# The head of a two-layer hybrid trunk as a written-out schedule, on one core

## The chip, the core and the metric

One Trainium2 chip, one of its cores. The metric is the device time of one execution, in microseconds (us). The core has a matrix engine (TensorE, PE in the profile), VectorE (DVE), ScalarE (ACT), GpSimd (POOL) and SyncE (SP), which issues all the transfers here. Each engine takes its instructions in the order in which they stand in its own queue; between engines they wait on semaphores.

## What is computed

Two layers over 256 tokens of width 1024, in float32. Each layer normalizes, makes one wide projection (9304 columns), runs three mixers on its parts (gated linear attention, sparse attention with an indexer, differential attention), projects each branch, merges them by gates and adds an output projection to the stream. x is 1 x 256 x 1024, DEPTH is 2, w_in is 1024 x 9304 a layer. y_a, y_b and y_c are the mixers' outputs, g the gates:

```python
def _rms(x, g=None):
    xf = x.astype(F32)
    y = xf * lax.rsqrt(jnp.mean(xf * xf, axis=-1, keepdims=True) + EPS)
    if g is not None:
        y = y * g.astype(F32)
    return y.astype(x.dtype)

def reference(x, norm_g, w_in, gla_wa2, gla_ba, gla_norm_g, dsa_qn_g, dsa_kn_g, diff_qn_g, diff_kn_g,
              diff_lq1, diff_lk1, diff_lq2, diff_lk2, w_br, w_out):
    B, T, _ = x.shape
    for l in range(DEPTH):
        h = _rms(x, norm_g[l])
        proj = h @ w_in[l]
        (gq, gk, gv, ga, gz, bq, bk, bv, iq, ik, iw, bz,
         cq, ck, cv, cz, gate) = jnp.split(proj, SPLIT_AT, axis=-1)
...
        merged = (g[:, :, 0] * (y_a @ w_br[l, 0])
                  + g[:, :, 1] * (y_b @ w_br[l, 1])
                  + g[:, :, 2] * (y_c @ w_br[l, 2]))
        x = x + merged @ w_out[l]
    return x
```

## The kernel before

**Tiles and products.** The 256 tokens are two tiles of 128 (t = 0, 1). A product in float32 is made of three products of split operands: each operand is a rounded part (hi) and a rest (lo), and `mm3` (L182) issues hi·hi, lo·hi and hi·lo, lines 183 to 185, into one PSUM tile of 128x512. Eight k tiles of 128 make up the depth of 1024, so a block of 512 columns takes 24 products for one t.

**Weights.** They come in 184 units (92 a layer) of 128x1024 float32, 512 KB: two k tiles of one block of 512 columns, so a block is four units. `Stream.need` (L137) issues the transfer of a unit into one of five `raw` buffers, and at L145 ScalarE copies it to `whi` and VectorE subtracts to get `wlo` (six buffers each). `need` runs up to 21 units ahead of its use; buffers coming free set when a transfer starts. The blocks go in the order of ORDER: bq, cq, ck, and so on.

**The head.** Ten idle products on zeros (WARM, L344) run first on PE. SP issues the two halves of x for t = 0 and the identity with the norm gains (`eyeg`, L350). For each t, `sumsq` (L208) squares and sums both halves on ScalarE; `norm_in` (L210) makes v on VectorE, its power -0.5 on GpSimd (L213), scales each half of x to h on VectorE (L217), transposes it on PE in four 128x128 pieces into one PSUM bank `hps` (L220), and copies each piece out: ScalarE writes hTh with the gain (L224), VectorE subtracts to hTl (L225). There are two banks for one t, k tiles 0 to 3 and 4 to 7. The first two units are asked for behind the head of t = 0 (FIRST), x of t = 1 behind them. `proj_first` (L254) does bq for t = 0, then two units of cq for t = 0 (AHEAD1), then bq for t = 1, then the rest of cq.

**What sets the order.** The code is written in this sequence, but a list scheduler behind it puts each engine's queue in an order of its own from its estimates of durations, within dependences. `tc.add_manual_dep` adds an order between two instructions without a semaphore; `ws.hold` (L128) uses it to keep the split of unit 3 of a layer behind the last copy of t = 0. Small tasks of the mixers (`Flow`) are put in between at counted places: `qk_task` normalizes bq's rows (L266 to L271, "qn") and transposes them (L278, "qkT"); `small_task` holds the indexer's keys and weights (L422 to L433, "ikh", "ikl", "iw", "iws"). `constants` (L312) makes masks, gains and scalars.

Of the kernel before, what the change touches and what calls it, by code (L numbers as in the profile page):

```python
# [65 lines left out]
def trunk(ctx: ExitStack, tc: tile.TileContext, x_in, units, wsmall, eye, pack, ptmp, wa2b, out):  # L66
# [57 lines left out]

    class Stream:
        def __init__(self):
            self.made, self.splits, self.after = [], [], {}
# [8 lines left out]

        def need(self, i, ahead=None):  # L137
            ahead = BUFS["ahead"] if ahead is None else ahead
            while len(self.made) < min(L * NUNIT, i + 1 + ahead):
                j = len(self.made)  # L140
                raw = wp.tile([P, 1024], F32, tag="raw", bufs=BUFS["raw"], name=nm("raw"))
                nc.sync.dma_start(raw, units[j])
                hi = wp.tile([P, 1024], F32R, tag="whi", bufs=BUFS["wt"], name=nm("whi"))
                lo = wp.tile([P, 1024], F32R, tag="wlo", bufs=BUFS["wt"], name=nm("wlo"))
                self.splits.append((A.activation(hi, raw, AF.Copy), V.tensor_sub(lo, raw, hi.bitcast(F32))))  # L145
                if j in self.after:
                    self.hold(j, self.after[j])
                self.made.append((hi.rearrange("p (k n) -> p k n", k=2), lo.rearrange("p (k n) -> p k n", k=2)))
# [61 lines left out]
    def norm_in(l, t):  # L210
        v, r = tiny(1, "v"), tiny(1, "r")
        V.scalar_tensor_tensor(v, ss[t][:, 0:1], EPS, ss[t][:, 1:2], op0=OP.add, op1=OP.add)
        G.tensor_tensor(r, v, half[:, :1], op=OP.pow)  # L213
        tt = slice(t * P, t * P + P)
        for hf in range(2):
            h = w2([P, 512], F32, "h")
            V.tensor_scalar_mul(h, x[:, t, HV[hf]], r)  # L217
            ps = at([P, 4, P], "hps")
            for j in range(4):
                TE.transpose(ps[:, j], h[:, j * P:(j + 1) * P], ident)  # L220
            for j in range(4):
                k = 4 * hf + j
                g = gT[:, l * KD8 + k:l * KD8 + k + 1]
                e = (A.activation(hTh[:, k, tt], ps[:, j], AF.Copy, scale=g),  # L224
                     V.scalar_tensor_tensor(hTl[:, k, tt], ps[:, j], g, hTh[:, k, tt].bitcast(F32),  # L225
                                            op0=OP.mult, op1=OP.subtract))
# [709 lines left out]
```

## Time and profile before

| | us |
|---|---|
| median of three timed runs | 612.82 |
| the three runs | 612.48, 612.82, 613.51 |
| the profiled execution's own time | 613.26 |
| its span in the profile | 611.5 |
| PE busy | 604.2 (99%) |
| VectorE busy | 434.1 (71%) |
| ScalarE busy | 354.0 (58%) |
| GpSimd busy | 63.0 (10%) |

The profiled execution took 613.26 us, of which the profile's span covers 611.5; the other 1.8 us lie around it. PE is busy nearly always, so what it does not do is read from single stretches: the list of what PE waited for, busy time by stretch with the granted clock beside it (1.00 is 2.4 GHz, 0.50 is 1.2 GHz), and each engine's timeline of the first tens of microseconds. PE's matmuls are pipelined: a duration of 0.39 us with starts 0.23 us apart means that the rate is 0.23.

### The profile page before, as it was taken

The page shows a single profiled execution, that of the slowest core. Times are in us where ns is not written, and L with a number is a line of the kernel's source. Part 1 is how long each engine was busy: PE and PEld are TensorE (multiplying, and loading weights), DVE is VectorE, ACT ScalarE, POOL GpSimd, SP SyncE. Part 2 cuts the span into 40 slices and gives each one's busy share as a digit, 9 for nine tenths or more (in the row PEclk, how much of TensorE's full clock was granted, in tenths as well). Part 3 has the DMA queues.
Part 4 walks back from the last instruction along what each step waited for, and adds up shares of the span by engine and source line. Part 5 has one row for each costly group of instructions (what it writes and reads, how often), then busy time and mean ns, then how long its engine had stood idle before and what let it go on. Part 6 is the DMA issues. An engine that isn't in the chain of part 4 may idle for free.

```text
span 611.5 us, 8711 instructions
## 1 busy us (share of the span) xinstructions
PE 604.2 (99%) x3180; PEld 507.3 (83%) x3180; DVE 434.1 (71%) x709; ACT 354.0 (58%) x612; POOL 63.0 (10%) x93
## 2 busy tenths in 40 slices
PE   7999999999999999999999999999999999999997
PEld 4788888898899888888878888889888988888886
DVE  5888657777989756648587776676888976575571
ACT  6778855766536754443466787576755555544430
POOL 2033101000022000000001340201000120000000
PEclk7999999999999999999999999999999999999999
DMA  8764565425534635555527455533554165455501
GB/s 319 279 208 138 173 206 173 138 104 173 173 103 167 190 129 198 177 194 181 172 87 244 152 161 183 195 115 104 184 167 166 48 230 158 152 177 201 178 30 70
DMA packets 28699, 100.85 MB, mean 165 GB/s; under 512 B 3184, under 2 KB 3696, under 8 KB 28656
## 3 DMA queue, kind: packets, MB, share of 16 engines
q1 hardware_dynamic: 28656, 100.30, 49.6%
q8 instruction: 25, 0.41, 0.3%
q14 instruction: 18, 0.15, 0.1%
HBM read 99.23 MB, written 1.05 MB: 164 GB/s over the span
## 4 chain that ended last, share of the span: by engine, by line
PE 97%; ACT 1%; DMA 1%; DVE 0%; SPq 0%; issue 0%
PE gate L183 7%; PE gate L184 7%; PE gate L185 7%; PE br L183 4%; PE br L184 4%; PE br L185 4%; PE out L185 2%; PE out L183 2%; PE out L184 2%; PE bz L185 1%; PE bz L183 1%; PE cq L183 1%; PE bz L184 1%; PE iq L183 1%; PE iq L185 1%; PE iq L184 1%
## 5 line engine op out<-in xcount | busy, mean ns | idle before, releaser
L145 DVE TENSOR_TENSOR wlo<-raw,whi 128x1024 fp32r<-128x1024 f32 x184 | 224.1, 1222 | 100.1 <-ACT whi L145 98.8
L145 ACT ACTIVATE whi<-raw 128x1024 fp32r<-128x1024 f32 x184 | 193.8, 1060 | 148.6 <-PE gate L185 39.6
L183 PE MATMUL gate<-whi,hTh 128*128 128x512 f32 x192 | 76.6, 399 | 0.0
L184 PE MATMUL gate<-wlo,hTh 128*128 128x512 f32 x192 | 76.1, 396 | 0.0
L185 PE MATMUL gate<-whi,hTl 128*128 128x512 f32 x192 | 75.9, 395 | 0.0
L185 PEld LDWEIGHTS gate<-whi,hTl 128*128 128x128 f32 x192 | 36.1, 188 | 8.1
L183 PEld LDWEIGHTS gate<-whi,hTh 128*128 128x128 f32 x192 | 36.1, 188 | 7.8
L184 PEld LDWEIGHTS gate<-wlo,hTh 128*128 128x128 f32 x192 | 36.2, 188 | 7.7
L190 POOL TENSOR_TENSOR r<-v,half 128x4 f32<-128x4 f32 (+1 forms) x24 | 34.2, 1424 | 2.0
L189 POOL TENSOR_SCALAR v<-ss 128x4 f32<-128x4 f32 (+1 forms) x24 | 11.8, 490 | 182.3 <-DVE ss L268 111.0
L183 PE MATMUL out<-whi,mTh 128*128 128x512 f32 (+1 forms) x72 | 26.7, 371 | 0.0
L184 PE MATMUL out<-wlo,mTh 128*128 128x512 f32 (+1 forms) x72 | 26.3, 366 | 0.0
L185 PE MATMUL out<-whi,mTl 128*128 128x512 f32 (+1 forms) x72 | 26.2, 366 | 0.0
L184 PE MATMUL br<-wlo,yTh 128*128 128x512 f32 x64 | 25.0, 390 | 0.0
L183 PE MATMUL br<-whi,yTh 128*128 128x512 f32 x64 | 25.0, 390 | 0.0
L185 PE MATMUL br<-whi,yTl 128*128 128x512 f32 x64 | 24.9, 389 | 0.0
L183 PE MATMUL iq<-hTh,whi 128*128 128x256 f32 x64 | 18.5, 289 | 0.0
L185 PE MATMUL bz<-hTh,wlo 128*128 128x256 f32 x64 | 18.2, 285 | 0.0
L184 PE MATMUL iq<-hTl,whi 128*128 128x256 f32 x64 | 18.2, 284 | 0.0
L183 PE MATMUL bz<-hTh,whi 128*128 128x256 f32 x64 | 18.1, 283 | 0.0
L184 PE MATMUL bz<-hTl,whi 128*128 128x256 f32 x64 | 18.0, 282 | 0.0
L185 PE MATMUL iq<-hTh,wlo 128*128 128x256 f32 x64 | 18.0, 281 | 0.0
(320 smaller groups left out, 1511.1 us busy)
## 6 DMA issues: line engine op xcount, KB each, us to landing
raw<-in_units SPq DMA_DIRECT2D x184, 512.0 KB, 3.4
x<-in_x SPq DMA_DIRECT2D x4, 256.0 KB, 4.5
wsr<-in_wsmall SPq DMA_DIRECT2D x2, 416.0 KB, 6.3
out<-x SPq DMA_DIRECT2D x3, 256.0 KB, 2.0
pt<-in_ptmp SPq DMA_DIRECT2D x1, 384.0 KB, 7.3
wa<-in_wa2b SPq DMA_DIRECT2D x1, 256.0 KB, 7.3
out<-x SPq DMA_DIRECT2D x2, 128.0 KB, 1.7
pk<-in_pack SPq DMA_DIRECT2D x1, 133.0 KB, 7.6
```

What stands on the lines that cost most here:

```text
L145: self.splits.append((A.activation(hi, raw, AF.Copy), V.tensor_sub(lo, raw, hi.bitcast(F32))))
L183: TE.matmul(ps, lh, rh, start=first, stop=False)
L184: TE.matmul(ps, lh, rl, start=False, stop=False)
L185: TE.matmul(ps, ll, rh, start=False, stop=last)
L189: G.tensor_scalar(v, ss, 1.0 / dim, EPS, op0=OP.mult, op1=OP.add)
L190: G.tensor_tensor(r, v, half[:, :n], op=OP.pow)
```

## The change

Only the head changes, and with it what the scheduler makes of the stretch behind it.

- Transfers: the first unit in two halves with `eyeg` between them; order x of t = 0, first half of unit 0, `eyeg`, second half, unit 1, unit 2, x of t = 1, unit 3.
- Units 0 to 3 are split by halves of 512 columns (one k tile each) over three engines: hi of units 0 and 2 on ScalarE, of 1 and 3 on GpSimd; lo on VectorE but for lo(0,1) and lo(2,1) on GpSimd. Here hi(j, h) is the hi part of half h of unit j.
- Square-and-sum of t = 0: one half on ScalarE, the other on VectorE by one fused instruction (`sumsq_v`).
- WARM is 12, and three idle products (FILL) stand behind the first eight transposes.
- `chain` fixes the order of the listed instructions on ScalarE, VectorE and GpSimd. The copies out of PSUM go k = 0 to 7, so four of one bank and then four of the other.
- AHEAD1 is 0 in the first layer: no cq between bq's t = 0 and t = 1.
- The instructions of `load_small` and `constants` on ScalarE and VectorE are issued behind the last copy of the head (`issue_after`), and unit 4's split is held behind it too.

```diff
-WARM = 10
-AHEAD1 = 2
-FIRST = 1
+WARM = 12
+FILL = 3
+AHEAD1 = (0, 2)
...
+        def load(self, between=None):
+            raw = wp.tile([P, 1024], F32, tag="raw", bufs=BUFS["raw"], name=nm("raw"))
+            i = units[len(self.raws)]
+            if between is None:
+                nc.sync.dma_start(raw, i)
+            else:
+                nc.sync.dma_start(raw[:, :512], i[:, :512])
+                between()
+                nc.sync.dma_start(raw[:, 512:], i[:, 512:])
+            self.raws.append(raw)
...
+    def order(a, b):
+        tc.add_manual_dep(a.ins, b.ins.name, NOSYNC, reason="order")
+
+    def sumsq_v(t, hf):
+        junk = w2([P, 512], F32, "junk")
+        xh = x[:, t, HV[hf]]
+        return V.tensor_tensor_reduce(junk, xh, xh, scale=1.0 / D, scalar=0.0, op0=OP.mult, op1=OP.add,
+                               accum_out=ss[t][:, hf:hf + 1])
...
+        n = AHEAD1[base > 0]
...
-    nc.sync.dma_start(eyeg, eye)
-    for t in range(2):
-        for h in range(2):
-            sumsq(t, h)
-        norm_in(0, t)
-        if t == 0:
-            ws.need(FIRST, 0)
-            xload(1)
+    ws.load(lambda: nc.sync.dma_start(eyeg, eye))
+    ws.load()
+    ws.load()
+    xload(1)
+    ws.load()
+    last = {}
+
+    def chain(e, ins):
+        if e in last:
+            order(ins, last[e])
+        last[e] = ins
+
+    wt = [ws.tiles() for _ in range(4)]
+
+    def hi(j, h, e):
+        c, dst, src = slice(512 * h, 512 * h + 512), wt[j][0], ws.raws[j]
+        chain(e, A.activation(dst[:, c], src[:, c], AF.Copy) if e == "A" else G.tensor_copy(dst[:, c], src[:, c]))
+
+    def lo(j, h, e):
+        c, (a, b) = slice(512 * h, 512 * h + 512), wt[j]
+        chain(e, (V if e == "V" else G).tensor_sub(b[:, c], ws.raws[j][:, c], a[:, c].bitcast(F32)))
...
+    def evacs(t, ps, *ks):
+        for k in ks:
+            a, b = evac(0, t, k, ps[k // 4])
+            chain("A", a)
+            chain("V", b)
+
+    chain("A", sumsq(0, 0))
+    chain("V", sumsq_v(0, 1))
+    hi(0, 0, "A")
+    hi(0, 1, "A")
+    r = scale(0)
+    hps = [scaled(0, hf, r) for hf in range(2)]
+    for _ in range(FILL):
+        order(TE.matmul(ps, idle[:, :P], idle, start=True, stop=True), hps[1][1])
+    hps = [a for a, _ in hps]
+    lo(0, 0, "V")
+    lo(0, 1, "G")
+    evacs(0, hps, 0, 1, 2, 3)
+    hi(1, 0, "G")
+    hi(1, 1, "G")
+    lo(1, 0, "V")
+    lo(1, 1, "V")
+    evacs(0, hps, 4, 5)
+    evacs(0, hps, 6)
+    evacs(0, hps, 7)
+    hi(2, 0, "A")
+    hi(2, 1, "A")
+    lo(2, 0, "V")
+    lo(2, 1, "G")
+    chain("A", sumsq(1, 0))
+    chain("A", sumsq(1, 1))
+    hi(3, 0, "G")
+    lo(3, 0, "V")
+    r = scale(1)
+    hi(3, 1, "G")
+    lo(3, 1, "V")
+    hps = [scaled(1, hf, r)[0] for hf in range(2)]
+    evacs(1, hps, *range(8))
+    ws.hold(4, (last["A"], last["V"]))
...
             if c == "bq":
-                load_small()
-                if l == 0:
-                    constants()
+                with ExitStack() as behind:
+                    if l == 0:
+                        for e in "AV":
+                            behind.enter_context(tc.issue_after(last[e].ins))
+                    load_small()
+                    if l == 0:
+                        constants()
```

`scale`, `scaled` and `evac` hold what `norm_in` did: v and the power; h and four transposes; the two copies of one k tile.

ScalarE's queue in the head, first of before and then of after, from the first weight unit on. `whi` is a unit's hi, `hTh` a copy out of a bank `hps` (its number tells the bank), `junk` a square-and-sum, and the brackets name the engine or transfer queue that is waited for.

```order
L145 ACTIVATE whi_142<-raw_140 128x1024 [waits DMAHW3_49]
L224 ACTIVATE hTh<-hps_112,eyeg 128x128 [waits PE_49]
L224 ACTIVATE hTh<-hps_127,eyeg 128x128 [waits PE_49]
L145 ACTIVATE whi_148<-raw_146 128x1024 [waits DMAHW4_49]
L208 ACTIVATE junk_154,ss_77<-x 128x512 [waits DMAHW5_49]
L224 ACTIVATE hTh<-hps_112,eyeg 128x128 [waits DVE_49]
L208 ACTIVATE junk_156,ss_77<-x 128x512 [waits DMAHW6_49,Activation_49]
L224 ACTIVATE hTh<-hps_127,eyeg 128x128 [waits DVE_49]
```

```order
L406 ACTIVATE whi_115<-raw_103 128x512 [waits DMAHW2_49]
L406 ACTIVATE whi_115<-raw_103 128x512 [waits DMAHW4_49]
L255 ACTIVATE hTh<-hps_135,eyeg 128x128 [waits DMAHW3_49,PE_49]
L255 ACTIVATE hTh<-hps_135,eyeg 128x128 [waits DVE_49] x3
L255 ACTIVATE hTh<-hps_142,eyeg 128x128 [waits PE_49]
L255 ACTIVATE hTh<-hps_142,eyeg 128x128 [waits DVE_49] x3
L406 ACTIVATE whi_119<-raw_109 128x512 [waits DMAHW6_49]
L406 ACTIVATE whi_119<-raw_109 128x512
L237 ACTIVATE junk_176,ss_77<-x 128x512 [waits DMAHW7_49]
L237 ACTIVATE junk_178,ss_77<-x 128x512 [waits DMAHW0_49,Activation_49]
```

Before, copies of the two banks and whole units alternate; after, the four copies of one bank stand together, each behind a wait for VectorE, then four of the other, and unit 2 and the squares of t = 1 stand behind all eight.

PE's queue from the last products of bq's third unit (before) and in bq's fourth unit (after) to its first ones for t = 1. bq_220 and bq_246 are the PSUM tiles of t = 0, bq_221 and bq_247 those of t = 1, cq_222 and cq_223 those of cq; `hps` is a transpose.

```order
L183 MATMUL bq_220<-whi_226,hTh 128x512
L184 MATMUL bq_220<-wlo_227,hTh 128x512
L185 MATMUL bq_220<-whi_226,hTl 128x512
L183 MATMUL bq_220<-whi_232,hTh 128x512
L183 MATMUL cq_222<-whi_238,hTh 128x512
L183 MATMUL bq_221<-whi_142,hTh 128x512
L184 MATMUL bq_221<-wlo_143,hTh 128x512
L185 MATMUL bq_221<-whi_142,hTl 128x512
L183 MATMUL cq_223<-whi_238,hTh 128x512
```

```order
L202 MATMUL bq_246<-whi_121,hTh 128x512
L203 MATMUL bq_246<-wlo_122,hTh 128x512
L204 MATMUL bq_246<-whi_121,hTl 128x512
L249 MATMUL hps_190<-eyeg,h_188 128x128 x4
L249 MATMUL hps_197<-eyeg,h_195 128x128 x4
L202 MATMUL bq_247<-whi_115,hTh 128x512
L203 MATMUL bq_247<-wlo_116,hTh 128x512
L204 MATMUL bq_247<-whi_115,hTl 128x512
```

Before, the transposes of t = 1 lie further ahead, between the second unit's products (20 products and 16 transposes stand ahead of the first of bq_221), and cq products lie among those of t = 1; after, they stand behind all 24 products of t = 0 with no cq product near.

VectorE's queue further on, where `small_task` and the rows of bq come: `iws` takes PE's `iw`, `ikl` the indexer's keys, `qn` is the normalized bq of one t, which PE then transposes.

```order
L271 TENSOR_TENSOR qn_531<-bq_220,r_528 128x512 [waits Pool_49]
L145 TENSOR_TENSOR wlo_269<-raw_266,whi_268 128x1024 [waits DMAHW2_49,Activation_49]
L145 TENSOR_TENSOR wlo_275<-raw_272,whi_274 128x1024 [waits DMAHW3_49,Activation_49]
L268 TENSOR_REDUCE ss_535<-sq_533 128x4 [waits Activation_49]
L425 TENSOR_TENSOR ikl_203<-small_487,ikh_202 64x256 [waits Activation_49]
L145 TENSOR_TENSOR wlo_281<-raw_278,whi_280 128x1024 [waits DMAHW4_49,Activation_49]
L428 TENSOR_TENSOR sml_201<-small_487,smh_200 104x256 [waits Activation_49]
L271 TENSOR_TENSOR qn_541<-bq_221,r_538 128x512 [waits DVE_49,Pool_49]
L145 TENSOR_TENSOR wlo_287<-raw_284,whi_286 128x1024 [waits DMAHW5_49,Activation_49]
L433 TENSOR_SCALAR iws_204<-iw_549 128x16 [waits PE_49]
```

```order
L375 TENSOR_TENSOR lamd_469<-lame_458 128x1 [waits Activation_49]
L307 TENSOR_REDUCE ss_527<-sq_525 128x4
L376 TENSOR_SCALAR nlam<-lamd_469 128x1 [waits DVE_49]
L537 TENSOR_SCALAR iws_230<-iw_563 128x16 [waits PE_49]
L529 TENSOR_TENSOR ikl_229<-small_486,ikh_228 64x256 [waits Activation_49]
L310 TENSOR_TENSOR qn_533<-bq_246,r_530 128x512 [waits Pool_49]
L158 TENSOR_TENSOR wlo_307<-raw_304,whi_306 128x1024 [waits DMAHW7_49,Activation_49]
L307 TENSOR_REDUCE ss_537<-sq_535 128x4 [waits Activation_49]
```

Before, qn of t = 0 stood well ahead of ikl and iws; after, iws and ikl stand ahead of it.

## Rows read from the trace of the kernel before

**Rows 1.** What PE waited for, whole run: us, times, longest.

```profile
PE hps L220 <- DVE h L217: 1.1, 1, 1.1
```

**Rows 2.** Busy time by stretch: stretch, us, PE busy (instructions), clock, DMA share, GB/s.

```profile
8.17:15.00 6.83, 6.22 (x18) 0.50 1.04 414
...
40.00:600.00 560.00, 559.77 (x2979) 1.00 0.48 158
```

**Rows 3.** PE's timeline, 12 to 18.5 us: start, duration, line, operation; idle before.

```profile
12.94 0.63 PE L185 MATMUL bq<-whi,hTl 128*128 128x512 f32 x1
13.37 1.83 PE L220 MATMUL hps<-eyeg,h 128*128 128x128 f32 x8
...
15.74 0.39 PE L183 MATMUL bq<-whi,hTh 128*128 128x512 f32 x1
15.97 0.39 PE L184 MATMUL bq<-wlo,hTh 128*128 128x512 f32 x1
...
17.82 0.50 PE L183 MATMUL cq<-whi,hTh 128*128 128x512 f32 x1 [0.28 <-ACT whi L145]
18.15 0.39 PE L183 MATMUL bq<-whi,hTh 128*128 128x512 f32 x1
```

**Rows 4.** SP's timeline, issue to landing (us), and ScalarE's first read of x.

```profile
1.64 0.42 SPq L350 DMA_DIRECT2D eyeg<-in_eye  x1
2.11 0.91 SPq L142 DMA_DIRECT2D raw<-in_units  x2
...
eyeg<-in_eye SPq DMA_DIRECT2D x1, 72.0 KB, 4.0
raw<-in_units SPq DMA_DIRECT2D x1, 512.0 KB, 5.1
raw<-in_units SPq DMA_DIRECT2D x1, 512.0 KB, 5.8
...
4.18 0.63 ACT L208 ACTIVATE junk<-x 128x512 bf16<-128x512 f32 x1
```

**Rows 5.** Timelines of ScalarE and VectorE: the copies out of PSUM.

```profile
8.17 0.61 ACT L224 ACTIVATE hTh<-hps,eyeg 128x128 fp32r<-128x128 f32 x2
...
14.46 0.37 ACT L224 ACTIVATE hTh<-hps,eyeg 128x128 fp32r<-128x128 f32 x1 [1.17 <-PE hps L220]
...
22.63 0.63 ACT L224 ACTIVATE hTh<-hps,eyeg 128x128 fp32r<-128x128 f32 x2 [0.52 <-DVE hTl L225]
...
14.86 0.35 DVE L225 SCALAR_TENSOR_TENSOR hTl<-hps,eyeg,hTh 128x128 fp32r<-128x128 f32 x1 [0.15 <-ACT hTh L224]
...
22.25 0.60 DVE L225 SCALAR_TENSOR_TENSOR hTl<-hps,eyeg,hTh 128x128 fp32r<-128x128 f32 x2
```

**Rows 6.** Groups by form: busy us, mean ns of one; idle before.

```profile
L833 POOL TENSOR_TENSOR gz<-gz,pk 128x512 f32<-128x512 f32 x4 | 4.4, 1093 | 24.7 <-DVE gz L291 17.8 <-issue 6.9
...
L751 POOL MEMSET ck<- 64x1024 f32 x4 | 3.8, 957 | 0.2
...
L213 POOL TENSOR_TENSOR r<-v,half 128x1 f32<-128x1 f32 x4 | 2.3, 563 | 116.3 <-DVE v L212 116.3
...
L315 DVE TENSOR_TENSOR wal<-wa,wah 128x512 fp32r<-128x512 f32 x1 | 0.7, 677 | 0.0
```

**Rows 7.** Timelines of PE and VectorE, 34 to 38 us.

```profile
37.71 0.34 PE L432 MATMUL iw<-eyeg,sm 104*128 104x104 f32 x2
37.89 0.60 PE L278 MATMUL qkT<-eyeg,qn 128*128 128x128 f32 x4
...
34.29 0.41 DVE L425 TENSOR_TENSOR ikl<-small,ikh 64x256 fp32r<-64x256 f32 x1
```

**Rows 8.** Timelines of GpSimd and VectorE, 34 to 42 us.

```profile
34.46 0.19 POOL L189 TENSOR_SCALAR v<-ss 128x4 f32<-128x4 f32 x1 [4.71 <-DVE ss L268]
...
40.69 1.29 POOL L189 TENSOR_SCALAR v<-ss 128x8 f32<-128x8 f32 x1 [4.93 <-DVE ss L268]
...
40.69 1.22 DVE L145 TENSOR_TENSOR wlo<-raw,whi 128x1024 fp32r<-128x1024 f32 x1
```

More of the change, by code (lines that the diff above doesn't have):

```diff
@@ L126, in __init__ @@
         def __init__(self):
-            self.made, self.splits, self.after = [], [], {}
+            self.raws, self.made, self.splits, self.after = [], [], {}, {}
         def hold(self, j, evac):
-            if j < len(self.splits):
+            if j in self.splits:
                 for a, b in zip(self.splits[j], evac):
@@ L135, in hold, with tiles, split @@
                 self.after[j] = evac
+        def load(self, between=None):
[8 more added lines that the diff above has]
+            self.raws.append(raw)
+        def tiles(self):
+            hi = wp.tile([P, 1024], F32R, tag="whi", bufs=BUFS["wt"], name=nm("whi"))
+            lo = wp.tile([P, 1024], F32R, tag="wlo", bufs=BUFS["wt"], name=nm("wlo"))
+            self.made.append((hi.rearrange("p (k n) -> p k n", k=2), lo.rearrange("p (k n) -> p k n", k=2)))
+            return hi, lo
+        def split(self):
+            j = len(self.made)
+            raw, (hi, lo) = self.raws[j], self.tiles()
+            self.splits[j] = (A.activation(hi, raw, AF.Copy), V.tensor_sub(lo, raw, hi.bitcast(F32)))
+            if j in self.after:
+                self.hold(j, self.after[j])
         def need(self, i, ahead=None):
@@ L139, in need @@
             while len(self.made) < min(L * NUNIT, i + 1 + ahead):
[L140 to L148, printed above, removed]
+                if len(self.raws) == len(self.made):
+                    self.load()
+                self.split()
             return self.made[i]
@@ L203, in trunk @@
     ss = [cp.tile([P, 2], F32, name=f"ss{t}") for t in range(2)]
+    def order(a, b):
[5 more added lines that the diff above has]
+                               accum_out=ss[t][:, hf:hf + 1])
     def sumsq(t, hf):
         junk = w2([P, 512], BF16, "junk")
-        A.activation(junk, x[:, t, HV[hf]], AF.Square, scale=1.0 / math.sqrt(D), accum_out=ss[t][:, hf:hf + 1])
+        return A.activation(junk, x[:, t, HV[hf]], AF.Square, scale=1.0 / math.sqrt(D), accum_out=ss[t][:, hf:hf + 1])
@@ new lines, in norm_scale, with norm_half @@
+    def norm_scale(t):
+        v, r = tiny(1, "v"), tiny(1, "r")
+        a = V.scalar_tensor_tensor(v, ss[t][:, 0:1], EPS, ss[t][:, 1:2], op0=OP.add, op1=OP.add)
+        return r, a, G.tensor_tensor(r, v, half[:, :1], op=OP.pow)
+    def norm_half(t, hf, r):
+        h = w2([P, 512], F32, "h")
+        a = V.tensor_scalar_mul(h, x[:, t, HV[hf]], r)
+        ps = at([P, 4, P], "hps")
+        for j in range(4):
+            b = TE.transpose(ps[:, j], h[:, j * P:(j + 1) * P], ident)
+        return ps, a, b
@@ L210, in norm_in, with evac @@
+    def evac(l, t, k, ps):
+        tt = slice(t * P, t * P + P)
+        g = gT[:, l * KD8 + k:l * KD8 + k + 1]
+        return (A.activation(hTh[:, k, tt], ps[:, k % 4], AF.Copy, scale=g),
+                V.scalar_tensor_tensor(hTl[:, k, tt], ps[:, k % 4], g, hTh[:, k, tt].bitcast(F32),
+                                       op0=OP.mult, op1=OP.subtract))
     def norm_in(l, t):
-        v, r = tiny(1, "v"), tiny(1, "r")
-        V.scalar_tensor_tensor(v, ss[t][:, 0:1], EPS, ss[t][:, 1:2], op0=OP.add, op1=OP.add)
@@ L213, in norm_in @@
-        G.tensor_tensor(r, v, half[:, :1], op=OP.pow)
-        tt = slice(t * P, t * P + P)
+        r, _, _ = norm_scale(t)
         for hf in range(2):
-            h = w2([P, 512], F32, "h")
-            V.tensor_scalar_mul(h, x[:, t, HV[hf]], r)
-            ps = at([P, 4, P], "hps")
+            ps, _, _ = norm_half(t, hf, r)
             for j in range(4):
[L220 to L226, printed above, removed]
+                e = evac(l, t, 4 * hf + j, ps)
@@ L257, in proj_first @@
         u0, u1 = base + UNIT[ORDER[0]], base + UNIT[ORDER[1]]
-        project([(p0, hT, u0, range(4), KD8, (0,)), (p1, hT, u1, range(AHEAD1), KD8, (0,)),
+        n = AHEAD1[base > 0]
+        project([(p0, hT, u0, range(4), KD8, (0,)), (p1, hT, u1, range(n), KD8, (0,)),
                  (p0, hT, u0, range(4), KD8, (1,))])
         yield p0
-        project([(p1, hT, u1, range(AHEAD1), KD8, (1,)), (p1, hT, u1, range(AHEAD1, 4), KD8, (0, 1))])
+        project([(p1, hT, u1, range(n), KD8, (1,)), (p1, hT, u1, range(n, 4), KD8, (0, 1))])
         yield p1
@@ L349, in trunk, with scale, scaled @@
     xload(0)
-    nc.sync.dma_start(eyeg, eye)
-    for t in range(2):
-        for h in range(2):
-            sumsq(t, h)
-        norm_in(0, t)
-        if t == 0:
-            ws.need(FIRST, 0)
-            xload(1)
+    ws.load(lambda: nc.sync.dma_start(eyeg, eye))
[15 more added lines that the diff above has]
+        chain(e, (V if e == "V" else G).tensor_sub(b[:, c], ws.raws[j][:, c], a[:, c].bitcast(F32)))
+    def scale(t):
+        r, a, b = norm_scale(t)
+        chain("V", a)
+        chain("G", b)
+        return r
+    def scaled(t, hf, r):
+        ps, a, b = norm_half(t, hf, r)
+        chain("V", a)
+        return ps, b
+    def evacs(t, ps, *ks):
[36 more added lines that the diff above has]
+    ws.hold(4, (last["A"], last["V"]))
     for l in range(L):
```

## The prediction

> **What bounds the kernel now.** I read the list of what PE waited for [rows 1], busy time and clock by stretch [rows 2], then PE's timeline of the first 20 us [rows 3]. From 40 to 600 us PE is busy for 559.77 of 560.00 us [rows 2]: the middle is a full queue of products, and whatever PE loses in the head is never won back. So the change is worth what it moves in the moment from which PE runs without a stop. Before, that moment is 18.15 us: the last gap is the 0.28 us ahead of 17.82, where PE waited for a ScalarE split [rows 3]. By 18.15, 20 products of 128x512 and all 16 transposes of the head are behind PE. Up to there PE was also slow: the granted clock is 0.50 (1.2 GHz) from 8.17 to 15.00 us [rows 2], products start 0.43 us apart (12.94, 13.37) instead of 0.23 (15.74, 15.97), and the eight transposes ahead of 14.93 take 1.83 us [rows 3], 0.21 each where the full clock would take half, 0.11.
>
> The sum is therefore one difference: when PE has N products behind it after the change, against before. Before, 50 products are reached at 18.15 + 30 x 0.23 = 25.1 us.
>
> **The transfers.** Before, the first weight unit is issued at 2.11 and lands 5.1 us later, at 7.2; the second, issued at about 2.58, after 5.8, at 8.4; the identity, issued at 1.64, after 4.0, at 5.6 [rows 4]. Now half a unit goes ahead of the identity and the other half behind it, so the bytes ahead of the second half are the same: I take 7.2 us for it, some 6.3 for the identity, 8.4 for the second unit, and for the third, which now goes ahead of the second half of x, 8.4 + 1.25 (a unit's share, 8.4 - 7.2) = 9.7. The identity came 1.4 us behind x, which ScalarE read at 4.18 [rows 4], though it is a seventh of a unit; if that stall goes away the half unit lands near 6.5, if it grows, near 7.7. Bounds: -0.7 and +0.5 us.
>
> **Square-and-sum on VectorE, more idle products, the fill.** PE stood 1.1 us ahead of the first transposes [rows 1]: two more idle products of 0.43 end inside that. The fused square-and-sum on VectorE is not in the trace; a two-input VectorE instruction of 128x512 took 0.68 [rows 6], which I take, and twice that is my upper bound. Its cover: ScalarE is held until 7.7 by the second half's copy, while the transposes end near 7.4, at the upper bound near 8.0: zero to 0.3. The three fill products run while PE would wait for that copy: zero.
>
> **The copies out of PSUM: the term that decides.** Each of the eight k tiles is copied by ScalarE and subtracted by VectorE, and in one PSUM bank the next copy waits for the last subtraction: at 22.63 ScalarE had stood idle 0.52 us until VectorE's hTl was done [rows 5]. The order before alternates two banks, so that two copies go at 8.17 in 0.61 us and two subtractions at 22.25 in 0.60 [rows 5]. The new order takes four k of one bank, then four of the other. A subtraction starts 0.40 us after its copy (14.46, 14.86), the next copy 0.38 after the subtraction's start (22.25, 22.63): 0.78 a pair, where two alternating banks need about 0.4.
> The Trainium skill, page "PSUM — Partial Sum Buffer", section "PSUM bank collisions raise a hardware error", says that two engines must not touch one bank at once and that the hardware neither arbitrates nor stalls. The trace agrees so far as a wait is there; the rule speaks against this order, and by it the sum is the one that the rows give.
>
> Step by step (a ScalarE pass over 128x512 takes 0.63 [rows 4]; the next starts 0.1 before its end, as two copies of 0.36 fit in 0.61 [rows 5]):
> - hi(0,1) 7.2 to 7.7; four pairs, 4 x 0.78, to 10.8. VectorE's queue then holds lo(1,0) and lo(1,1), 0.60 each to the next start: 12.0. GpSimd has made hi(1,*) by 10.1 (lo(0,1), then two casts): hidden.
> - Fifth subtraction from 12.0, three more pairs: ScalarE's last copy lets go at 14.2. Only behind it stands hi(2,0), though its data came at 9.7: done 14.8, k4's product at 14.85. Before, k4 started at 15.74 with eight more transposes done [rows 3], 0.9 us of work: so far it is even.
> - hi(2,1) to 15.3; lo(2,1) on GpSimd, priced by its two-input instruction of this size, 1.09 [rows 6]: 16.45. Bounds 0.68 (VectorE's) and 1.77 (rival c).
> - hi(3,0), a GpSimd cast, is not in the trace. Its memset of 64x1024 took 0.96, so half of it, 0.5, is the lower bound, the two-input 1.09 the upper; a cast reads one input, so 0.55, near the memset: 17.0. VectorE's lo(3,0) to 17.7, v to 17.85, GpSimd's power 0.56 [rows 6] to 18.45, and only behind it hi(3,1) to 19.0, lo(3,1) to 19.65.
> - h follows on VectorE to 20.5. PE ends bq's first tile at 20.2, the eight transposes at 21.0. ScalarE does bq's squares first, then copies from 20.85; first product of t = 1 at 21.25. AHEAD1 is 0 here, so PE has nothing to put between, where before cq products filled in.
> - Four pairs pace four k, 4 x 0.78 = 3.1; then four at PE's own 0.70: 48 products done at 27.2.
> - cq's first unit waits in ScalarE's queue behind all copies: 26.1 to 27.2; VectorE's subtraction 1.22 [rows 8], to 28.45. PE puts two products in and waits: at 28.5 it has 50 behind it.
> - The constants' instructions now stand behind the copies; VectorE's five small ones fall into its wait for that unit (26.5 to 27.2): zero.
>
> 28.5 - 25.1 = **3.4 us** lost.
>
> **The later order.** VectorE's iws, which waits for PE's iw transposes, and ikl now stand ahead of bq's qn, and PE has the qkT transposes right behind iw. Before, PE went from iw at 37.71 to qkT at 37.89 without a wait [rows 7], since qn had been made earlier. Now PE waits for some 0.1 (iws), 0.4 (ikl [rows 7]), 0.68 (qn, as any two-input 128x512) and three hand-overs of 0.04: 1.3; ScalarE's ikh in between may add 0.2. I take **1.4**, at least 1.1, since the three are in line. The weight ring has five buffers and refills from 12 us on, so the units behind have landed when they are needed; I see no further gap.
>
> Together 3.4 + 1.4 = 4.8 us on the profiled execution's 613.26: 618.1. That execution is 0.44 above the median of the three runs (612.82), so the median to expect is **617.6**.
>
> **Rivals.**
> (a) *Not slower: the copies do not take turns.* If ScalarE's copies ran 0.25 apart as at 8.17 [rows 5], the eighth would let go at 9.75 instead of 14.2, just as the third unit lands; the chain up to t = 1's first product would come some 4.3 sooner, and t = 1 would not be paced (1.1 less): 617.6 - 5.4 = 612.2, no change. It decides if the second copy starts less than 0.5 us after the first. Against it: the waits stand in the built order, and rows 5 show one at work. 0.08.
> (b) *Faster: PE's clock was the bound.* If the fill products hold the full clock and the data are there in time, the head saves 9 products x 0.20 + 8 transposes x 0.10 = 2.6 us: 610.2. It decides if PE never waits over 0.5 us between 8 and 20 us. Against it: every step above waits for another engine. 0.05. The Trainium skill, page "TensorE: Matmul & The Clock Gate", section "Why this matters for your kernels", says that idle gaps between products halve the clock; by that rule the fill products bring this gain, and rows 2 agree as far as the 0.50 behind the idle time at 7 to 8 us.
> (c) *Much slower: GpSimd and the clock.* GpSimd's small instruction took 0.19 at 34.46 but 1.29 at 40.69, about as long as VectorE subtracted there, 1.22 [rows 8]. If each of lo(2,1) and the two casts on the path is held up for one VectorE half, 0.68, that is up to 2.0 us. And if the gaps keep 1.2 GHz beyond 20 us, eight transposes cost 0.8 more and a k of t = 1 1.28 instead of 0.78, some 1.5 together. Price 2 to 3.5: 619.6 to 621.1. 0.17. The Trainium skill, page "GPSIMD Engine Reference", section "1. Specifications", says that GpSimd shares its SBUF interfaces with VectorE's two-input instructions; the trace agrees with 1.29 beside 0.19.
> (d) *The plan does what it says in part:* transfers early and GpSimd quick (-0.7, -0.4, -0.1, the late gap -0.3): 616.1. That lies in the forecast's own range.
>
> **How the numbers follow.** Forecast, 617.6 (616.0 to 619.5): 0.70, with (d). Rivals (a) 0.08, (b) 0.05, (c) 0.17. The range leaves out (a), (b) and the far end of (c): 615.8 to 620.3. About 0.2% is what a measurement of this kernel can tell from no change. Faster 0.05, same 0.08, slower 0.87.
>
> **What would show it.** In the profile after: ScalarE's hTh starts 0.78 apart in fours; hi of the third unit near 14.2, long after it landed; PE idle near 14, 19 and 28 us, and 1.4 us between iw and qkT near 42; no idle worth naming after that. A PE without gaps from 12 us on, or copies 0.25 apart, proves me wrong. Gaps of the right kind with other lengths mean that a price is off, most likely that of a GpSimd cast or the landing of the first half unit.

## The result

| | before | after |
|---|---|---|
| median, us | 612.82 (five runs, 612.28 to 613.51) | 618.33 (five runs, 618.12 to 618.91) |
| profiled execution, us | 613.26 | 618.26 |
| its span, us | 611.5 | 616.5 |
| last product of PE starts at, us | 608.07 | 613.16 |
| first product of the third block, ck, us | 39.26 | 44.24 |

The change makes the kernel slower by 0.97% (ratio 1.0097, interval 1.0086 to 1.0107), 5.5 us; 617.6 had been forecast, with a range of 615.8 to 620.3. All of it is lost in the first 45 us: PE's first product on ck comes 4.98 us later than before, its last product 5.09 us later, and between the two PE takes 568.8 us before and 568.9 after.

What PE waited for in the kernel after (us in all, times, longest). `bq` is written by the products of the first block, `hps` by the transposes, `whi` and `wlo` are the hi and lo of a weight unit:

```profile
PE bq L202 <- ACT whi L406: 1.9, 1, 1.9
PE bq L203 <- DVE wlo L410: 1.6, 3, 1.2
PE qkT L317 <- DVE qn L310: 1.3, 1, 1.3
...
PE hps L249 <- DVE h L246: 0.9, 1, 0.9
PE cq L203 <- DVE wlo L158: 0.5, 1, 0.5
```

Before, beside the 1.1 us of [rows 1] and the 0.28 us of [rows 3], PE's longest waits in the head were for copies out of PSUM, and ck began at 39.26:

```profile
PE bq L183 <- ACT hTh L224: 1.3, 2, 1.1
```

```profile
39.26 0.39 PE L183 MATMUL ck<-whi,hTh 128*128 128x512 f32 x1
```

PE by stretch (stretch, us, busy, granted clock, DMA share, GB/s), to be held against [rows 2]:

```profile
8.17:15.00 6.83, 3.71 (x14) 1.00 1.03 401
15.00:18.00 3.00, 2.78 (x7) 0.50 0.99 378
...
45.00:600.00 555.00, 554.78 (x2948) 1.00 0.49 159
```

From 8.17 to 15 us the clock is now 1.00 where it was 0.50, and PE is busy for 3.71 us where it was 6.22, for about the same work: 12 products begin in it, where before 10 products and eight transposes did. What the faster products saved became waits. From 45 us on the clock is full as before. This compares one execution of each kernel: over a whole execution the mean clock on record is 0.994 to 1.00 for the kernel before and 0.994 to 0.997 in the five executions of the kernel after.

ScalarE's copies out of PSUM, VectorE's subtractions of unit 1, and GpSimd's part (start, duration, operation, count, idle before):

```profile
7.45 0.35 ACT L255 ACTIVATE hTh<-hps,eyeg 128x128 fp32r<-128x128 f32 x1
8.22 0.37 ACT L255 ACTIVATE hTh<-hps,eyeg 128x128 fp32r<-128x128 f32 x1 [0.42 <-DVE hTl L256]
...
12.05 0.37 ACT L255 ACTIVATE hTh<-hps,eyeg 128x128 fp32r<-128x128 f32 x1 [1.62 <-DVE hTl L256]
...
13.89 1.14 ACT L406 ACTIVATE whi<-raw 128x512 fp32r<-128x512 f32 x2
...
20.99 0.36 ACT L255 ACTIVATE hTh<-hps,eyeg 128x128 fp32r<-128x128 f32 x1
```

```profile
10.47 1.28 DVE L410 TENSOR_TENSOR wlo<-raw,whi 128x512 fp32r<-128x512 f32 x2
```

```profile
7.62 1.28 POOL L410 TENSOR_TENSOR wlo<-raw,whi 128x512 fp32r<-128x512 f32 x1 [1.62 <-ACT whi L406]
...
15.11 1.28 POOL L410 TENSOR_TENSOR wlo<-raw,whi 128x512 fp32r<-128x512 f32 x1 [5.09 <-ACT whi L406]
16.32 0.62 POOL L406 CAST whi<-raw 128x512 fp32r<-128x512 f32 x1
17.82 0.56 POOL L242 TENSOR_TENSOR r<-v,half 128x1 f32<-128x1 f32 x1 [0.87 <-DVE v L241]
18.33 0.61 POOL L406 CAST whi<-raw 128x512 fp32r<-128x512 f32 x1
```

The copies of one bank start 0.77 to 0.79 apart, each after 0.42 us of idle time until VectorE's subtraction is done: the wait of [rows 5], now from copy to copy. The 1.62 us ahead of 12.05 are the same wait with unit 1's two subtractions (10.47 to 11.75) in VectorE's queue ahead of the fifth tile's. Unit 2's hi (13.89) stands behind all eight. From 15.11 GpSimd subtracts, casts, makes the power and casts again, one behind the other, while VectorE waits (1.74 and 1.25 us); PE, at half clock up to 18.2 us, waits for 0.2 us at a time there.

PE's products at the ends of its waits:

```profile
11.20 0.50 PE L203 MATMUL bq<-wlo,hTh 128*128 128x512 f32 x1 [1.20 <-DVE wlo L410]
...
14.56 0.51 PE L202 MATMUL bq<-whi,hTh 128*128 128x512 f32 x1 [1.92 <-ACT whi L406]
...
19.00 0.50 PE L202 MATMUL bq<-whi,hTh 128*128 128x512 f32 x1 [0.19 <-POOL whi L406]
...
27.37 0.69 PE L202 MATMUL cq<-whi,hTh 128*128 128x512 f32 x2
28.60 0.50 PE L203 MATMUL cq<-wlo,hTh 128*128 128x512 f32 x1 [0.54 <-DVE wlo L158]
...
42.19 0.34 PE L536 MATMUL iw<-eyeg,sm 104*128 104x104 f32 x2
43.83 0.66 PE L317 MATMUL qkT<-eyeg,qn 128*128 128x128 f32 x4 [1.29 <-DVE qn L310]
44.24 0.48 PE L202 MATMUL ck<-whi,hTh 128*128 128x512 f32 x1
```

These are the forecast's gaps near 14, 19 and 28 us, and the one between iw and qkT. The 1.20 us ahead of 11.20 was not named there; unit 2's hi, at the end of ScalarE's copies, comes later than it anyway.

### The profile page after: what moved, and what is told of

Read it like the earlier page. It is cut to its first block, busy times and chain, and to the rows that moved or that the text cites. A ratio compares the mean times of both kernels' runs of the same rounds, so it can differ in the third digit from the quotient of the medians.

```text
span 616.5 us, 8732 instructions
## 1 busy us (share of the span) xinstructions
PE 605.5 (98%) x3185; PEld 506.4 (82%) x3185; DVE 434.8 (71%) x713; ACT 352.1 (57%) x610; POOL 64.3 (10%) x99
## 4 chain that ended last, share of the span: by engine, by line
PE 95%; DVE 1%; ACT 1%; DMA 1%; POOL 0%; issue 0%; SPq 0%; ACTq 0%
PE gate L202 7%; PE gate L203 7%; PE gate L204 7%; PE br L203 4%; PE br L202 4%; PE br L204 4%; PE out L204 2%; PE out L203 2%; PE out L202 2%; PE bz L204 1%; PE bz L202 1%; PE cq L203 1%; PE iq L204 1%; PE iq L202 1%; PE bz L203 1%; PE iq L203 1%
## 5 line engine op out<-in xcount | busy, mean ns | idle before, releaser
L158 DVE TENSOR_TENSOR wlo<-raw,whi 128x1024 fp32r<-128x1024 f32 x180 | 219.0, 1222 | 95.8 <-ACT whi L158 94.3
L158 ACT ACTIVATE whi<-raw 128x1024 fp32r<-128x1024 f32 x180 | 189.1, 1059 | 144.1 <-PE gate L204 39.8
L209 POOL TENSOR_TENSOR r<-v,half 128x4 f32<-128x4 f32 (+1 forms) x24 | 32.6, 1357 | 2.0
L208 POOL TENSOR_SCALAR v<-ss 128x4 f32<-128x4 f32 (+1 forms) x24 | 9.8, 407 | 181.8 <-DVE ss L307 105.5
L202 PE MATMUL iq<-hTh,whi 128*128 128x256 f32 x64 | 18.5, 289 | 0.0
L204 PE MATMUL bz<-hTh,wlo 128*128 128x256 f32 x64 | 18.2, 285 | 0.0
L203 PE MATMUL iq<-hTl,whi 128*128 128x256 f32 x64 | 18.2, 284 | 0.0
```

What stands on the lines that cost most here:

```text
L158: self.splits[j] = (A.activation(hi, raw, AF.Copy), V.tensor_sub(lo, raw, hi.bitcast(F32)))
L202: TE.matmul(ps, lh, rh, start=first, stop=False)
L203: TE.matmul(ps, lh, rl, start=False, stop=False)
L204: TE.matmul(ps, ll, rh, start=False, stop=last)
L208: G.tensor_scalar(v, ss, 1.0 / dim, EPS, op0=OP.mult, op1=OP.add)
L209: G.tensor_tensor(r, v, half[:, :n], op=OP.pow)
```

## The experiments

The theory: three things make the loss, the copies that take turns within one bank, a chain over GpSimd behind them, and the late order on VectorE; the clock and the early transfers change little or help. The rivals: the clock (case b of the prediction), the order of the copies as such, and waits that hide one another. As a measure beside the medians I use the start of PE's first product on ck, since behind it the kernels take the same time: 568.8 to 569.0 us to the last product in eleven of the twelve traces, and 569.5 in that of run 6.

**1. Even and odd k tiles in two banks.** The order of the copies stays.

```diff
-        ps = at([P, 4, P], "hps")
         for j in range(4):
-            b = TE.transpose(ps[:, j], h[:, j * P:(j + 1) * P], ident)
+            k = 4 * hf + j
+            b = TE.transpose(banks[k % 2][:, k // 2], h[:, j * P:(j + 1) * P], ident)
...
-            a, b = evac(0, t, k, ps[k // 4])
+            a, b = evac(0, t, k, ps[k % 2], k // 2)
```

> The changed kernel with one edit: the eight transposes of a token tile go to the two PSUM banks by turns (even k tiles in one, odd in the other) instead of four and four; the order of the copies, k = 0 to 7, stays. Theory (in one bank a ScalarE copy waits for the VectorE subtraction ahead of it): copies start about 0.4 us apart instead of 0.785; unit 2's hi is done some 2 us sooner than 14.5 us, the first product of t = 1 starts near 19.8 instead of 21.4 and runs without pacing, and the 0.5 us wait at cq goes. With the queues as they are built here (the late order comes out as in the kernel before, so the 1.3 us ahead of qkT go too) some 4.0 us of the 5.5 come back: 614.3 us, 613.6 to 615.2. Rival (the order of the copies is not what paces; the hand-overs between the engines or the splits are): copies stay 0.78 apart, 618 us.

Measured: 614.09 us, 1.0023 of before (1.0014 to 1.0031); 4.2 us of the 5.5 are back. ScalarE's copies, which now come two at a time:

```profile
7.98 0.63 ACT L261 ACTIVATE hTh<-hps,eyeg 128x128 fp32r<-128x128 f32 x2 [0.50 <-PE hps L254]
8.77 0.63 ACT L261 ACTIVATE hTh<-hps,eyeg 128x128 fp32r<-128x128 f32 x2 [0.16 <-DVE hTl L262]
...
11.59 0.63 ACT L261 ACTIVATE hTh<-hps,eyeg 128x128 fp32r<-128x128 f32 x2 [1.40 <-DVE hTl L262]
12.12 1.14 ACT L412 ACTIVATE whi<-raw 128x512 fp32r<-128x512 f32 x2
```

and PE (the first product on unit 2, the first for t = 1, cq, ck):

```profile
12.79 0.49 PE L202 MATMUL bq<-whi,hTh 128*128 128x512 f32 x1 [0.61 <-ACT whi L412]
...
19.92 0.50 PE L202 MATMUL bq<-whi,hTh 128*128 128x512 f32 x1 [0.35 <-ACT hTh L261]
...
25.60 0.64 PE L202 MATMUL cq<-whi,hTh 128*128 128x512 f32 x2
...
40.12 0.47 PE L202 MATMUL ck<-whi,hTh 128*128 128x512 f32 x1
```

Two copies take 0.79 us, so 0.39 each; unit 2 is met at 12.79 instead of 14.56, t = 1 starts at 19.92 instead of 21.41 and runs at 0.23 a product, and at cq there is no wait left: the product behind the first 50 starts at 26.07 instead of 28.60. That is 2.5 us, and it is net: in this execution the first copy came 0.53 us later (7.98 instead of 7.45), of which 0.38 is there already at VectorE's first read of x. Then VectorE's queue came out with qn ahead of iws, and the 1.29 us ahead of qkT are gone too; ck starts at 40.12, 4.1 us sooner. So this run shows the turn's price of some 2.5 us in the head, and that the late wait went with it, but not by itself what the late order costs.

**2. The late order alone.** qn of t = 0 (`q`) ahead of unit 12's subtraction on VectorE; QN is 12.

```diff
+        if not normed:
+            order(ws.splits[QN][1], q)
+        normed.append(q)
```

> The changed kernel with one more order on VectorE: the normalized bq of t = 0 (qn) stands ahead of the subtraction of unit 12, so ahead of ikl and iws. Theory (the late order costs a wait of its own, and it adds to the head's loss): PE's 1.29 us ahead of the qkT transposes near 43 us go, nothing else moves: 618.3 - 1.3 = 617.0 us, 616.6 to 617.4. Rival (PE's loss is set by units that come late anyway, and the wait moves to the next block): 618.3 us, with the 1.3 us standing ahead of another product before 60 us.

Measured: 616.70 us, 1.0067 (1.0055 to 1.0079), 1.6 us below the changed kernel. The qkT transposes follow iw without a wait, and the head's waits of 1.9, 1.2 and 0.5 us stay:

```profile
42.07 0.34 PE L542 MATMUL iw<-eyeg,sm 104*128 104x104 f32 x2
42.26 0.60 PE L323 MATMUL qkT<-eyeg,qn 128*128 128x128 f32 x4
42.61 0.48 PE L203 MATMUL ck<-whi,hTh 128*128 128x512 f32 x1
```

ck starts at 42.61, 1.63 us sooner. Of these, 1.51 lie between iw and ck (0.54 us here, 42.19 to 44.24 in the kernel after), and 0.12 were there at iw, what is left of an earlier start. So the late order costs 1.5 us: the wait of 1.29, and 0.2 that stopping and starting PE adds to the starts around it. The wait did not move to another place.

**3. Without the three fill products.**

```diff
-FILL = 3
+FILL = 0
```

> The changed kernel without the three idle products behind the first transposes. Theory (every step of the head waits for another engine, so the clock of the first products is worth nothing): if the clock falls, the twelve products of k tiles 0 to 3 take longer, but that goes off the waits of 1.2 and 1.9 us that follow them: 618.3 us, 617.9 to 618.8. Rival (the full clock that the fill products keep is worth the 12 x 0.2 us): 620.7 us.

Measured: 618.60 us (618.21 to 619.41; 1.0100, 1.0085 to 1.0114), no difference from 618.33 that can be told. The clock is full from 8.17 to 13 us without the fill products too; the low clock comes sooner and lasts longer, and no loss shows:

```profile
8.17:13.00 4.83, 3.05 (x11) 1.00 1.01 398
13.00:19.80 6.80, 5.45 (x11) 0.50 0.98 379
```

**4. Before, with the idle products.** 12 instead of 10, and three behind the first transposes.

```diff
+            if l == 0 and t == 0 and hf == 1:
+                for _ in range(FILL):
+                    m = TE.matmul(idle_ps, idle[:, :P], idle, start=True, stop=True)
+                    tc.add_manual_dep(m.ins, b.ins.name, NOSYNC, reason="order")
```

> The kernel before with one part of the change: 12 idle products instead of 10, and the three behind the first eight transposes. Theory (the copies and splits pace the head of before too; a faster PE waits for them): granted clock 1.00 between 8 and 13 us, waits in place of slow products, 612.8 us plus up to 0.6 for products that come out in another order: 612.5 to 613.5. Rival (the clock is what bounds before's head, the 2.6 us of the prediction's case of a gain): 610.2 us.

Measured: 612.72 us (twelve runs, 612.22 to 615.50), 1.0007 (0.9995 to 1.0019): no gain. In the profiled execution, a long one of 615.09 us, the clock was full to 11.6 us and 0.50 from there to 18.4:

```profile
8.17:11.60 3.43, 1.85 (x6) 1.00 1.03 417
11.60:18.40 6.80, 5.95 (x17) 0.50 1.03 413
```

While it was full PE was busy for 1.85 of 3.43 us; it waited 1.07 us for a copy. At half clock it was busy for 5.95 of 6.80 us, with waits of 0.56 and 0.29.

The twelve times follow the mean clock of the execution: 612.22 to 612.77 in the seven with 1.00 (0.999 in one), 613.56 and 613.99 with 0.997, 614.99 to 615.50 in the three with 0.994. So the seven at full clock stay 2 us above the 610.2 of case (b): where every product waits for a copy or a split, a fast PE waits longer. But the low clock is not free where PE has products ready: half of the 5.95 us, as an estimate of what it cost there, is 3.0, about what the three executions with 0.994 are longer by. In the kernel before less goes with it: its 65 executions beside these runs have a median of 613.3 with 0.994 (20) and of 612.5 with 1.00 (16). Why the clock falls in one execution and not in another is open.

**5. Unit 3's casts on ScalarE.**

```diff
-    hi(3, 0, "G")
+    hi(3, 0, "A")
...
-    hi(3, 1, "G")
+    hi(3, 1, "A")
```

> The changed kernel with the two hi halves of unit 3 on ScalarE instead of GpSimd; all else as it is. Theory (between 15 and 20 us the chain on GpSimd, its subtraction, cast, power and second cast, is what PE waits for): both casts are done on ScalarE by 17.2 us, where it idles from 16.2 on; VectorE's v and the power no longer stand between them, so t = 1 starts some 0.8 us sooner and everything behind follows: 617.5 us, 617.0 to 618.0. Rival (the VectorE queue, not GpSimd, sets the end of t = 0): 618.3 us.

Measured: 617.62 us (617.15 to 618.74), 1.0083 (1.007 to 1.0096), 0.7 us below the changed kernel; the two waits at unit 3 (0.19 and 0.22 us ahead of 19.00 and 19.73) are gone. But its profiled execution, 618.74, has the second half unit 0.75 us late (ScalarE at 7.67 instead of 6.92) and PE at half clock to 20.7 us, running products 0.43 us apart without a stop, so that there the waits may be gone because PE is slower. The size rests on the medians, and the two intervals overlap (the kernel after: 1.0086 to 1.0107): the median is the expected one, but a gain clear of noise is not shown.

**6. Before, with the copies in order by banks.**

```diff
+                e0 = None if l or k == 0 else e
...
+                if e0:
+                    for a, b in zip(e, e0):
+                        tc.add_manual_dep(a.ins, b.ins.name, NOSYNC, reason="order")
```

> The kernel before with the copies out of PSUM held in the changed kernel's order, k = 0 to 3 of one bank and then 4 to 7 of the other; the scheduler places everything else. Theory (a turn of 0.785 us costs only where nothing else stands between two copies of a bank): the scheduler puts splits, squares and the copies of the other token tile between them, and PE has products of other blocks for the gaps: 613.0 us, 612.5 to 613.7. Rival (the order by banks costs by itself, eight copies at 0.785 instead of 0.4 for each token tile): 3 us or more above before, 615.8 us.

Measured: 613.25 us, 1.0010 (1.0001 to 1.0019). ScalarE's queue there:

```profile
7.50 0.35 ACT L225 ACTIVATE hTh<-hps,eyeg 128x128 fp32r<-128x128 f32 x1
8.34 1.06 ACT L145 ACTIVATE whi<-raw 128x1024 fp32r<-128x1024 f32 x1 [0.49 <-DMA raw<-in_units]
...
9.92 0.35 ACT L225 ACTIVATE hTh<-hps,eyeg 128x128 fp32r<-128x128 f32 x1
10.17 0.62 ACT L208 ACTIVATE junk<-x 128x512 bf16<-128x512 f32 x1
...
10.96 0.37 ACT L225 ACTIVATE hTh<-hps,eyeg 128x128 fp32r<-128x128 f32 x1
```

Between the first copies of a bank stand a split or a square, so the wait for VectorE is filled. The order by banks costs 0.5 us where a scheduler may fill the turns, by an interval that just leaves out nothing at all, and some 2.5 in the kernel after, where `chain` forbids it. The two kernels differ in more than that (AHEAD1, the halves), so the comparison is of sizes only.

**7. The transfers of before.** The identity first, unit 0 whole, x of t = 1 ahead of unit 2.

```diff
-    ws.load(lambda: nc.sync.dma_start(eyeg, eye))
-    ws.load()
+    nc.sync.dma_start(eyeg, eye)
+    ws.load()
     ws.load()
     xload(1)
     ws.load()
+    ws.load()
```

> The changed kernel with the transfers in the order of the kernel before: the identity first, unit 0 in one piece, x of t = 1 ahead of unit 2. Theory (the transfers are a part that works: hi(0,1) is done 0.7 us sooner by them, and it stands ahead of the whole chain of copies): the first copy starts at 8.2 instead of 7.45 us and the whole chain with it, 619.0 us, 618.5 to 619.3. Rival (the early unit is hidden behind the waits that come later, as the clock was): 618.3 us.

Measured: 619.43 us (618.64 to 620.04), 1.0109 (1.0095 to 1.0123), 1.1 us above the changed kernel. In the profiled execution the first copy starts at 7.77 instead of 7.45 us and ck at 45.15 instead of 44.24. That is more than the expected 0.7, and above the expected range (618.5 to 619.3). The trace shows 0.3 us of it at the first copy and at the first product on unit 2 (14.86 instead of 14.56). By the transposes of t = 1 it is 0.7 (21.02 instead of 20.30): the clock is 0.50 up to 20.8 us here, up to 18.2 in the kernel after, and the last products of the tile run slower for it. The wait ahead of qkT, 1.44 instead of 1.29 us, makes most of the rest. Three of the four executions here have a mean clock of 0.994, but two of five in the kernel after. The one with 0.997 took 618.64 us, against 618.12 to 618.33 for those of the kernel after at 0.996 and 0.997. So between 0.3 and 1.1 us belong to the transfers, and how much of it is the clock's is not shown.

**8 to 10. The plan without its three costs.** From experiment 1: all hi on ScalarE, each half put between copies, t = 1's h ahead of unit 3, and lo(3,1) on GpSimd. AHEAD1 stays 0.

```diff
-    evacs(0, hps, 0, 1, 2, 3)
-    hi(1, 0, "G")
-    hi(1, 1, "G")
-    lo(1, 0, "V")
-    lo(1, 1, "V")
-    evacs(0, hps, 4, 5)
-    evacs(0, hps, 6)
-    evacs(0, hps, 7)
-    hi(2, 0, "A")
-    hi(2, 1, "A")
-    lo(2, 0, "V")
-    lo(2, 1, "G")
+    evacs(0, hps0, 0, 1)
+    hi(1, 0, "A")
+    evacs(0, hps0, 2)
+    lo(1, 0, "V")
+    hi(1, 1, "A")
+    evacs(0, hps0, 3)
+    lo(1, 1, "V")
+    evacs(0, hps0, 4)
+    hi(2, 0, "A")
+    evacs(0, hps0, 5)
+    lo(2, 0, "V")
+    hi(2, 1, "A")
+    lo(2, 1, "G")
+    evacs(0, hps0, 6)
+    evacs(0, hps0, 7)
...
-    lo(3, 1, "V")
+    lo(3, 1, "G")
...
```

> The changed kernel with even and odd k tiles in two banks, and the written-out order changed: all hi on ScalarE, each half put between two copies instead of behind all eight (hi(1,0) behind k1's copy, hi(1,1) behind k3's, hi(2,0) behind k4's, hi(2,1) behind k5's), lo(0,1), lo(2,1) and lo(3,1) on GpSimd, the squares, v and h of t = 1 ahead of unit 3. Theory (with the turns and the casts gone the same plan is worth what it should be): gaps of 0.1 to 0.7 us are left, some 2.0 in all between 8 and 16 us, the first product of t = 1 starts before 17 us, the late wait is gone: 611.3 us, 610.7 to 612.0. Rival (transfers or VectorE set the end whatever the order is): 613 us or more.

Measured: 612.31 us, 0.9994 of before (0.9985 to 1.0003): not told from before, and above the expected range (610.7 to 612.0). It is 6.0 us below the changed kernel. The longest wait that is left names the place, and VectorE's and GpSimd's timelines show what happens there:

```profile
PE hps L254 <- DVE h L246: 1.5, 3, 0.8
```

```profile
14.46 1.89 DVE L246 TENSOR_SCALAR h<-x,r 128x512 f32<-128x512 f32 x2 [0.68 <-POOL r L242]
```

The same two by their line (shortest, middle and longest in ns, first and last start):

```profile
L246 DVE TENSOR_SCALAR h<-x,r x2: 486/988/1491, 14.5 to 14.9; 128x512 f32<-128x512 f32 x2
```

GpSimd:

```profile
11.93 1.70 POOL L416 TENSOR_TENSOR wlo<-raw,whi 128x512 fp32r<-128x512 f32 x1 [2.56 <-ACT whi L412]
13.86 0.56 POOL L242 TENSOR_TENSOR r<-v,half 128x1 f32<-128x1 f32 x1 [0.24 <-DVE v L241]
14.71 1.36 POOL L416 TENSOR_TENSOR wlo<-raw,whi 128x512 fp32r<-128x512 f32 x1 [0.28 <-ACT whi L412]
```

The two h of t = 1, 0.88 us together in the kernel after, took 1.89: 0.49 the first, 1.49 the second, which started at 14.9 and ended at 16.35, 0.3 us behind GpSimd's lo(3,1) (14.71 to 16.07). The ninth run moves that one subtraction to VectorE.

```diff
-    lo(3, 1, "G")
+    lo(3, 1, "V")
```

> The kernel of the eighth experiment with one subtraction, lo(3,1), on VectorE instead of GpSimd. In the eighth VectorE's second h of t = 1 took 1.49 us, beside 0.49 for the first, and it ended when GpSimd's lo(3,1) did. Theory (VectorE's h is held up while GpSimd subtracts): both h take 0.49, the second four transposes start near 15.4 instead of 16.41, 0.9 us come back, of which 0.3 may go to the wait at qkT near 36 us, which the queues as they are built here leave open: 611.6 us, 611.2 to 612.0. Rival (the second h waits for its half of x or for something else): it takes 1.5 us again, 612.3 us.

Measured: 611.37 us, 0.9981 (0.9972 to 0.9990): faster than before. The two h, and ck at 37.32 us where it was 38.46:

```profile
14.11 0.88 DVE L246 TENSOR_SCALAR h<-x,r 128x512 f32<-128x512 f32 x2 [0.68 <-POOL r L242]
14.90 1.29 DVE L416 TENSOR_TENSOR wlo<-raw,whi 128x512 fp32r<-128x512 f32 x2
```

So GpSimd's instruction held VectorE's up. The Trainium skill, page "SBUF — State Buffer", section "SBUF: two separate sides", says that GpSimd shares a pair of ports with VectorE's instructions that run in a 2-port mode or have two inputs in SBUF, and that the first one holds the pair for its whole instruction while the other is blocked. The trace agrees in that the second h lasted until 0.3 us behind the end of GpSimd's instruction; that h, with one input, runs in such a mode is shown by no row. Not every VectorE instruction was held up: its subtractions out of PSUM at 7.84 and 8.62 us in the kernel after took 0.35 us, as ever, beside GpSimd's of 7.62 to 8.90.

The tenth adds the second's edit to the ninth.

> The ninth experiment with the order of the second on top (qn of t = 0 ahead of unit 12's subtraction on VectorE). Theory: the two effects are separate, the 0.3 us at qkT go and nothing else moves: 611.3 us, 610.9 to 611.7, below the kernel before by 0.15 to 0.3%. Rival (the late wait is no longer there to win): as the ninth, 611.6 us.

Measured: 611.42 us, 0.9977 (0.9968 to 0.9987), the same as the ninth within noise. In the ninth's trace some 0.3 us of the late wait were still there; a product stands between iw and qkT, and qkT starts 0.54 us behind it where the rate is 0.23:

```profile
36.37 0.47 PE L204 MATMUL cq<-whi,hTl 128*128 128x512 f32 x1
36.91 0.66 PE L323 MATMUL qkT<-eyeg,qn 128*128 128x128 f32 x4
```

In the tenth's trace they are gone, but its transposes of t = 1 begin at 15.20 instead of 14.65 us, and ck at 37.56 instead of 37.32. So the medians decide neither for the theory nor for the rival. Against the 612.99 us of before in the same runs the ninth kernel is 1.6 us faster; its mean clock is 1.00, and its waits on the way to 24 us are 0.2 to 0.3 us each.

No run puts the cq products back between the two tiles (AHEAD1) or undoes VectorE's square-and-sum or the later constants by themselves. Runs 8 to 10 keep all three and are no slower than before, so none of them has to be a loss; what cq products would have filled in the kernel after is not measured.

## Why the prediction was right

Each step of the sum can be read in the trace after. Forecast and measured, in us:

| step | forecast | measured |
|---|---|---|
| hi(0,1) done, first copy starts | 7.7 | 7.45 |
| from copy to copy in one bank | 0.78 | 0.77 to 0.79 |
| first product on unit 2 | 14.85 | 14.56 |
| lo(2,1) on GpSimd | 1.09 | 1.28 |
| a cast of 128x512 on GpSimd | 0.55 | 0.61 |
| hi(3,1) done | 19.0 | 18.94 |
| first product of t = 1 | 21.25 | 21.41 |
| 48 products done, cq begins | 27.2 | 27.37 |
| 50 products behind PE | 28.5 | 28.60 |
| head, against 25.1 before | 3.4 | 3.5 |
| wait between iw and qkT | 1.4 | 1.29 (1.5 from iw to ck) |

- **The transfers and the first copy.** The second half unit was there at 6.92, 0.3 us sooner than I took; it came inside the given bound of -0.7. (The 4.18 us that I set the identity against is ScalarE's read of the second half of x; it read the first at 3.50, so the distance of 1.4 us that I took for a stall is not one between landings.) That lead was spent by 19 us on GpSimd's subtraction, taken from another shape of output and 0.2 too short. Two small errors of opposite sign, so the end is better than its parts.
- **The copies, the deciding term,** were right in mechanism and size (run 1), and so was what hangs on them: unit 2's hi behind all eight copies though its data had long landed.
- **The GpSimd chain** was right as a place in the trace: its last cast ends at 18.94, and PE, which has waited 0.19 us for it, goes on at 19.00. Its worth as a sum is not shown clear of noise (run 5: 0.7 us of the medians). Of rival (c), GpSimd held up by VectorE, the trace after shows nothing: both subtractions took 1.28 us. (Its two rows are of 128x4 and 128x8; a 128x8 took 0.20 us at 54.70 in the kernel before, so the size is not what made 1.29.) The contention is real: in run 8 GpSimd's took 1.70 beside VectorE's, and VectorE's h was held up. The other half of (c), the low clock beyond 15 us, came (0.50 at 15 to 18 us) and cost nothing in this execution, since PE still waited 0.19 us behind it.
- **The late order** was right: a wait of 1.29 us in the trace, 1.5 us by the starts from iw to ck, and run 2 took it away without another wait in its place.
- **The median.** The spans differ by 5.0 us, which is the measured 3.5 of the head and 1.5 of the late order; the forecast's terms were 3.4 and 1.4. The medians differ by 5.5, since the profiled execution of before lay 0.44 above its median and that of after 0.07 below. My 617.6 took 0.44 off, as if the execution after would lie as far above its median, and is 0.7 short: 0.2 by the terms and 0.5 by that.
- **Rival (a)** fell with the copies at 0.78. **Rival (b)** fell with PE's waits of 1.20 and 1.92 us between 8 and 20 us, and with run 4, where executions at full clock took 612.2 to 612.8 us, not 610.2. Its price per transpose at half clock, 0.21 us, is 0.195 by the starts (13.37 to 14.93), which changes nothing here.

## What to carry to other kernels

Where two engines read one PSUM bank in turn, spread neighbouring tiles over two banks before writing an order out by hand: the same order of copies took 0.39 instead of 0.78 us a tile here. A fixed order takes away the scheduler's means of filling such turns, so what it wins must be worth more than such turns cost, here some 2.5 us. And a faster clock, or data that come sooner, is worth what the next wait leaves of it: find that wait first.
